# Short products and the group norm's remainder put at other places of a block of 256 tokens

## The chip, the cores and the metric

The kernel runs on 1 of the 8 cores of a Trainium2 chip. The metric is the device time of one execution in microseconds (us), the median of the runs.

## What is computed

One layer on 4096 tokens of 1024 features. `h` is the RMS-normalised input with a scale and a shift; one projection `h @ w_in` feeds a pooling branch and an RWKV-7 branch; the branches, each with a SiLU gate, are concatenated, go through `w_out`, are added to `x`, and a last RMSNorm follows. The RWKV branch, with 8 heads of 64, is the part that matters here:

```
r, w_lo, k, v, a_lo, z = split(seg)              # after a token shift
decay = exp(-exp(-softplus(-(w0 + tanh(w_lo) @ w_up)) - 0.5))
a  = sigmoid(a0 + a_lo @ a_up)
kk = normalise(k * k_k);  k = k * (1 + (a - 1) * k_a)
S_t = S_{t-1} (diag(decay_t) - kk_t^T (a_t kk_t)) + v_t^T k_t;   y_t = S_t r_t
y  = (y - mean) * rsqrt(var + eps) * ln_w + ln_b      # per head: the group norm
y_rwkv = (y + sum(r * k * r_k) * v) * silu(z)         # the sum is the bonus
```

## The kernel before

A first phase (to about 400 us) computes `h` and the pooling branch. The second, which the change touches, takes the tokens in 16 blocks of 256, each of 4 chunks of 64, and a last one projects with `w_out`.

In the second phase two things run side by side. **front(b+1)** (L536) prepares the next block. It computes 17 segments of the projection (`seg`, L550), 24 products of 128x257 each, into PSUM tiles `pj` of a pool of three buffers; segment 0 is `lo`, and each head pair p = 0 to 3 has four: 1+4p is k (`kS`), 2+4p r (`rS`), 3+4p v (`vS`), 4+4p z (`zS`). Tiles are called by segment here: pj_9 is the k segment of pair 2. The two operations at L561 (ScalarE) and L562 (VectorE) empty a `pj`. Front is a generator; `fill(n)` runs n of its steps, three products each, between the parts of the current block. Between the steps of a segment it also issues short products, from lists in `mid` by step number:

- `lowrank` (L588): products `pl` and `pa` (L591, L592), ScalarE's tanh `tw` and `ta` and an addition (L593 to L595), VectorE's scan `L` (L596), two exponentials `Ppad` and `Pi` (L597, L598). It runs in the v segment.
- `bonus` (L632): product `pb` (L634), then `bon` (L635). It needs `rk` (L615).
- `cent` (L622): products `vps` (L625) and two copies (L627). It needs `vS` only.

Their PSUM tiles come from the pool of `pj` too. For the last pair the two are left over in `f["todo"]` and run in `scores` of the next block.

**The current block** runs `scores` (L649; products `scp_0` to `scp_3` at L663, their masking at L670, copies at L678), `inverse` (L698; VectorE's recurrence of 30 pairs L727, L732 from the transposition `Ab`, L709, to the transpositions `UV`, `MQ`, L745, L746; then `qp`, L756, and `m21p`, L764, on TensorE, behind 20 steps of front and the product `lead`, L790), and `chain` (L796). In each chunk chain runs L815 with the state `S`, copies `xa` (L822), products `psn` (L827), copies `UV` (L835), the state's product `psn` (L843) with its renewal (L849), the output's product (L854) and copies `y` (L861).

After two chunks `gn` (L868) normalises y: square, sum (L871 to L874), a power on GpSimd (L876), the norm's product (L878), and `gn_out` (L885): four transpositions `ytp` (L890), copies `mx` (L892), two operations (L893, L894) and a DMA. gn is a generator of three parts; `run(gns[0], 1)` runs the next part where it stands. `ytp` shares a pool of two PSUM buffers with `scp_sc`, `d2p`, `btp` and `qp`.

Tile's scheduler sets the order of each engine's instructions: by the order of the code, with some parts moved ahead by 400 places (`tc.high_priority(offset=PRI)`), and an instruction that can't run yet by the scheduler's own account gives way to a later one. Each engine then runs its list strictly in this order.

Of the kernel before, what the change touches and what calls it, by code (L numbers as in the profile page):

```python
# [52 lines left out]
def kernel(  # L53
# [426 lines left out]
    with ExitStack() as ph:  # L480
# [56 lines left out]
        def front(b, f):  # L537
# [7 lines left out]
                    hx += [ht[:, k, :] for k in range(4)]  # L545


            mid = {3: [], 6: []}

            def seg(m, name, bufs=2):  # L550
                pp = ps_pj.tile([P, TB2 + 1], F32, tag="pj", name=f"pj{b}_{m}")
# [25 lines left out]
            for p in range(NPAIR):  # L577
# [19 lines left out]
                    A.activation(Pp[:, :, 1:], c3(L), AF.Exp, bias=0.0, scale=cexp)  # L597
                    A.activation(Pi, L, AF.Exp, bias=0.0, scale=-cexp)  # L598

                mid[3].append(lowrank)  # L600
                yield
                vS = yield from seg(3 + 4 * p, "vS")
                if p == 0:
# [36 lines left out]
                        PE.matmul(pn[32 * q : 32 * q + 32, :], hsel, sqs[q], start=True, stop=True)  # L640
                    A.copy(ssb, pn)

                mid[6] += [cent, bonus]
                if p < NPAIR - 1:
                    yield
            f["todo"] = [norms] + mid[6]
# [2 lines left out]
        def scores(b, f, fill):  # L649
            AR, BK = f["AR"], f["BK"]  # L650

            d2 = sm.tile([64, NI], F32, tag="d2", name=f"d2_{b}")
            d2T = sm.tile([P, 32], F32, tag="d2T", name=f"d2T{b}")
            sc = blk.tile([P, NI, P], F32, tag="sc", name=f"sc{b}")
            BT = blk.tile([P, NCH, 512], F32, tag="BT", name=f"BT{b}")
            stg = f["stg"] = f["UV"][0:64].rearrange("q c e -> q (c e)")[:, 0:1024].rearrange("q (t i) -> q t i", t=32)
            for ch in range(NCH):

                pts = [pool.tile([P, 512], F32, tag=tg, name=f"scp{b}_{ch}_{tg}") for pool, tg in ((ps_sc, "sc"), (ps_x, "px"))]
                for j in range(4):  # L660
                    for hq in range(2):
                        o = 64 * hq
                        PE.matmul(  # L663
                            pts[hq][:, j * P : (j + 1) * P],
                            BK[o : o + 64, j, ch].rearrange("q a t -> q (a t)"),
                            AR[o : o + 64, j, ch].rearrange("q a t -> q (a t)"),
                            start=True, stop=True,
                        )
                for hq in range(2):
                    V.tensor_mul(  # L670
                        sc[:, ch * NH : (ch + 1) * NH, :].rearrange("q (j h) t -> q j h t", h=2)[:, :, hq],
                        pts[hq].rearrange("q (j t) -> q j t", j=4),
                        mask.unsqueeze(1).to_broadcast([P, 4, P]),
                    )

                for kb in range(2):
                    o, i8 = 32 * kb, slice(ch * NH, (ch + 1) * NH)
                    A.copy(stg[o : o + 32, :, i8], sc[o : o + 32, i8, o : o + 32].rearrange("q i t -> q t i"))  # L678
                fill(FS + 1)
                if ch == 2:  # L680
                    pt = ps_sc.tile([P, 512], F32, tag="sc", name=f"d2p{b}")
                    for c_ in range(NCH):
                        PE.transpose(pt[:64, c_ * P : (c_ + 1) * P], ssb[:, c_ * C : (c_ + 1) * C], ident)
                    V.tensor_scalar_max(
                        d2.rearrange("q (c p h) -> q c p h", c=NCH, h=2),
                        pt[:64].rearrange("q (c p e) -> q c p e", c=NCH, e=32)[:, :, :, 0:2], L2_EPS * L2_EPS,
                    )
                    V.reciprocal(d2, d2)
                    for g in range(2):
                        V.transpose(d2T[64 * g : 64 * g + 64], d2)  # L690
                if ch != 2:
                    f["todo"].pop(0)()
                fill(FS)
                if ch % 2 == 0:
                    run(gns[0], 1)
            f["sc"], f["BT"], f["d2T"] = sc, BT, d2T

        def inverse(b, f, fill):  # L698
# [71 lines left out]
        def ordered(mm):  # L770

            pin[0] = True
            return tc.keep_in_program_order(mm)
# [22 lines left out]
        def chain(b, f, fill):  # L796
            AR, UV, sc, BT, pc = f["AR"], f["UV"], f["sc"], f["BT"], f["pc"]
            MT = UV[0:64].rearrange("q c (h t) -> q (c h) t", h=NH)
            pe, po = f["px"]
            uo = 4 * HS  # L800
            for ch in range(NCH):
                par = 256 * (ch % 2)

                psn = ps_s.tile([P, 512], F32, tag="psn", name=f"psn{b}_{ch}")
                if ch % 2 == 0:
                    y = blk.tile([P, 512], F32, tag="y", name=f"y{b}_{ch}", bufs=3)
                yv = y[64 * (ch % 2) : 64 * (ch % 2) + 64].rearrange("q (j f e) -> q j f e", f=2, e=HS)
                uv = UV[0:64, ch, :].rearrange("q (j f e) -> q j f e", f=2, e=HS)

                for p in range(NPAIR):  # L810
                    cs = slice(par + p * HS, par + (p + 1) * HS)
                    for ar in range(2):
                        for hf, px in ((0, pe), (1, po)):
                            o, ro = 64 * hf, 64 * (hf ^ ar)
                            ordered(PE.matmul(  # L815
                                px[ro : ro + 64, cs], AR[o : o + 64, p, ch, ar, :], S[o : o + 64, p, :],
                                start=(p == 0 and ar == 1), stop=(ar == 0), skip_group_check=True,
                            ))
                xa = blk.tile([64, 2, 256], F32, tag="W", name=f"xa{b}_{ch}")
                for hf, px in ((0, pe), (1, po)):  # L820
                    with tc.high_priority(offset=PRI):
                        A.copy(xa[:, hf, :], px[64 * hf : 64 * hf + 64, par : par + 256])  # L822
                fill(FA)
                nl = lead(b, f, ch + 1) if ch + 1 < NCH else iter(())
                for p in range(NPAIR):
                    for hf in range(2):
                        ordered(PE.matmul(  # L827
                            psn[64 * hf : 64 * hf + 64, uo + p * HS : uo + (p + 1) * HS],
                            MT[:, ch * NH + 2 * p + hf, :], xa[:, hf, p * HS : (p + 1) * HS],
                            start=True, stop=True, skip_group_check=True,  # L830
                        ))
                    run(nl, 1)
                for hf in range(2):
                    with tc.high_priority(offset=PRI):
                        A.copy(uv[:, :, hf], psn[64 * hf : 64 * hf + 64, uo:].rearrange("q (j e) -> q j e", e=HS))  # L835
                run(gns[0], 1)

                Sd = blk.tile([P, NPAIR, HS], F32, tag="Wt", name=f"Sd{b}_{ch}")
                V.tensor_mul(Sd, S, pc[:, :, ch : ch + 1].to_broadcast([P, NPAIR, HS]))
                fill(FB)  # L840
                for h in range(NH):
                    o, e = 64 * (h % 2), slice(h * HS, (h + 1) * HS)
                    ordered(PE.matmul(  # L843
                        psn[o : o + 64, (h // 2) * HS : (h // 2 + 1) * HS], BT[:, ch, e], UV[:, ch, e],
                        start=True, stop=True, skip_group_check=True,
                    ))
                with tc.high_priority(offset=PRI):
                    for p in range(NPAIR):
                        V.scalar_tensor_tensor(  # L849
                            S[:, p, :], psn[:, p * HS : (p + 1) * HS], pc[:, p, ch : ch + 1], Sd[:, p, :], op0=ALU.mult, op1=ALU.add,  # L850
                        )
                for h in range(NH):
                    hf, o = h % 2, 64 * (1 - h % 2)
                    ordered(PE.matmul(  # L854
                        (pe, po)[hf][o : o + 64, par + (h // 2) * HS : par + (h // 2 + 1) * HS],
                        sc[:, ch * NH + h, 64:128], UV[:, ch, h * HS : (h + 1) * HS],
                        start=False, stop=True, skip_group_check=True,
                    ))
                for hf, px in ((0, pe), (1, po)):
                    o = 64 * (1 - hf)  # L860
                    A.copy(yv[:, :, hf], px[o : o + 64, par : par + 256].rearrange("q (j e) -> q j e", e=HS))  # L861
                run(gns[0])
                if ch % 2 == 1:
                    gns[0] = gn(b, f, ch // 2, y)
                    run(gns[0], 1)
                fill(FY)
# [49 lines left out]
        def run(g, n=100000):  # L916
            for _ in range(n):
                if next(g, run) is run:
                    return
# [48 lines left out]
        gns = [iter(())]  # L968
        fs = {0: {}}
        run(front(0, fs[0]))  # L970
        for b in range(NB2):
            f = fs[b]
# [80 lines left out]
```

## Time and profile before

| | |
|---|---|
| median of 3 runs | 2112.47 us (2110.70 to 2113.29) |
| the profiled execution, its own time | 2114.03 us |
| its span, first to last instruction | 2112.3 us |
| TensorE busy (PE) | 1979.8 us, 94%, 20186 matmuls |
| VectorE (DVE) / ScalarE (ACT) / GpSimd (POOL) | 1404.4 / 1045.7 / 130.8 us |
| granted TensorE clock, mean | 0.984 |
| the chain of work that ended last | PE 47%, DVE 31%, ACT 13% |

A matmul's busy time in the profile includes its way through the array, so back-to-back matmuls overlap: a 128x257 product is shown with 0.27 us and the next one starts 0.11 us later. The PE column is therefore full while PE's idle times, shown in brackets, are short of the truth by the overlap. "L843 <- ACT UV L835" says what ended an idle time. A clock of 1.00 is 2.4 GHz, 0.50 is 1.2 GHz.

### The profile page before, as it was taken

Reading aid. Unit: us, or ns where it says so; the run is one execution under the profiler, and the core shown is the slowest. Engines: PE = TensorE matmul, PEld = TensorE weight load, DVE = VectorE, ACT = ScalarE, POOL = GpSimd, SP = SyncE. Lnnn points to the kernel's source line nnn. Section 1 sums busy time; section 2 is a strip of 40 time slices with the busy share of each in tenths; the row PEclk is TensorE's granted clock in tenths of the full one; section 3 lists DMA queues with packets and bytes.
Section 4 is the critical chain, followed back from the end, with each engine's and each line's share of the span. In section 5 each row is a group of like instructions: output and inputs, shape, how many; then the busy total and the mean of one; then the engine's idle time right before and its main releaser. Section 6 shows DMA issues by size and latency. Waiting matters only on the chain.

```text
span 2112.3 us, 48406 instructions
## 1 busy us (share of the span) xinstructions
PE 1979.8 (94%) x20186; PEld 1460.1 (69%) x20186; DVE 1404.4 (66%) x3533; ACT 1045.7 (50%) x2247; POOL 130.8 (6%) x262
## 2 busy tenths in 40 slices
PE   5999999999999999999999999999999989999998
PEld 2444444687777777777777777777777767788886
DVE  7898987466857757668577676685675766533333
ACT  3555433355565565655655656556556553322211
POOL 0000000000000000000000000000000000100000
PEclk8999999999999999999999999999999999999999
DMA  8867767200110110101101101011011334433422
GB/s 311 277 224 240 241 216 271 68 21 2 32 32 2 31 27 7 32 4 30 32 2 31 27 7 32 3 30 32 2 31 31 131 112 139 165 136 133 155 96 74
DMA packets 140445, 183.20 MB, mean 87 GB/s; under 512 B 12097, under 2 KB 94017, under 8 KB 140226
## 3 DMA queue, kind: packets, MB, share of 16 engines
q1 hardware_dynamic: 140226, 180.11, 25.9%
q8 instruction: 158, 2.59, 0.5%
q14 instruction: 61, 0.50, 0.1%
HBM read 121.22 MB, written 58.85 MB: 85 GB/s over the span
## 4 chain that ended last, share of the span: by engine, by line
PE 47%; DVE 31%; ACT 13%; issue 4%; DMA 2%; POOL 1%; SPq 0%; ACTq 0%; DVEq 0%; POOLq 0%
PE po L953 6%; PE po L955 6%; PE po L954 6%; DVE Wt L727 5%; DVE W L732 4%; PE pp L412 4%; PE pp L411 4%; PE pp L410 4%; PE pj L557 3%; PE pj L558 2%; PE pj L559 2%; DVE sc L670 2%; PE scp_sc L663 2%; DVE L L596 2%; ACT UV L678 2%
## 5 line engine op out<-in xcount | busy, mean ns | idle before, releaser
L557 PE MATMUL pj<-hh,w2h 128*128 128x257 f16 x2176 | 604.3, 278 | 14.3 <-DVE kS L562 13.5
L559 PE MATMUL pj<-hh,w2l 128*128 128x257 f16 x2176 | 598.1, 275 | 0.0
L558 PE MATMUL pj<-hl,w2h 128*128 128x257 f16 x2176 | 596.6, 274 | 0.0
L557 PEld LDWEIGHTS <-w2h 128*128 128x128 f16 x2176 | 213.1, 98 | 69.1 <-issue 27.4
L558 PEld LDWEIGHTS <-w2h 128*128 128x128 f16 x2176 | 215.6, 99 | 47.8 <-issue 17.0
L559 PEld LDWEIGHTS <-w2l 128*128 128x128 f16 x2176 | 211.7, 97 | 31.7
L953 PE MATMUL po<-wo,mh 128*128 128x512 f32 x512 | 204.6, 400 | 2.4 <-ACT mh L937 2.4
L954 PE MATMUL po<-wo,mh 128*128 128x512 f32 x512 | 202.1, 395 | 0.0
L411 PE MATMUL pp<-lo,w1h 128*128 128x512 f16 x512 | 194.0, 379 | 1.4 <-DVE lo L225 1.4
L410 PE MATMUL pp<-hi,w1h 128*128 128x512 f16 x512 | 194.1, 380 | 0.6 <-ACT hi L224 0.6
L412 PE MATMUL pp<-hi,w1l 128*128 128x512 f16 x512 | 194.0, 379 | 0.0
L957 DVE TENSOR_TENSOR x<-po,x 128x512 f32<-128x512 f32 x64 | 44.2, 691 | 155.8 <-PE po L955 155.7
L959 ACT ACTIVATE sq<-x 128x512 f32<-128x512 f32 x64 | 40.4, 631 | 212.0 <-DVE x L957 194.9
L727 DVE TENSOR_TENSOR Wt<-W,Ab 128x30 f32<-128x30 f32 (+7 forms) x480 | 118.5, 247 | 13.7 <-ACT Ab L711 3.1
L732 DVE TENSOR_TENSOR W<-W,Wt 128x30 f32<-128x30 f32 (+7 forms) x480 | 117.9, 246 | 8.8
L953 PEld LDWEIGHTS po<-wo,mh 128*128 128x128 f32 x512 | 97.0, 189 | 24.6 <-ACT mh L937 2.6
L954 PEld LDWEIGHTS po<-wo,mh 128*128 128x128 f32 x512 | 96.8, 189 | 22.2
L678 ACT COPY UV<-sc 32x256 f32<-32x256 f32 x128 | 81.5, 637 | 48.4 <-DVE sc L670 46.3
L955 PE MATMUL po<-wo,ml 128*128 128x512 f32 x256 | 101.6, 398 | 0.0
L562 DVE SCALAR_TENSOR_TENSOR kS<-pj,c,kS 128x256 f32<-128x256 f32 x64 | 30.2, 471 | 103.4 <-ACT kS L561 102.9
L412 PEld LDWEIGHTS <-w1l 128*128 128x128 f16 x512 | 50.1, 98 | 61.6 <-issue 2.0
L410 PEld LDWEIGHTS <-w1h 128*128 128x128 f16 x512 | 50.2, 98 | 59.0 <-issue 0.8
(244 smaller groups left out, 3815.1 us busy)
## 6 DMA issues: line engine op xcount, KB each, us to landing
x<-in_x_dram SPq DMA_DIRECT2D x64, 256.0 KB, 3.1
out_dram<-x SPq DMA_DIRECT2D x64, 256.0 KB, 2.0
xk<-in_xT_dram SPq DMA_DIRECT2D x56, 256.0 KB, 4.1
xt<-in_x_dram SPq DMA_DIRECT2D x28, 512.0 KB, 5.7
wada<-in_w_ada_dram SPq DMA_DIRECT2D x24, 512.0 KB, 6.7
w2raw<-in_w_in_dram SPq DMA_DIRECT2D x17, 512.0 KB, 6.0
hh<-hT_hi SPq DMA_DIRECT2D x32, 257.0 KB, 4.1
hl<-hT_lo SPq DMA_DIRECT2D x32, 257.0 KB, 3.3
```

The source lines that it names most:

```text
L410: PE.matmul(pp, w1_hi[m][:, k, :], hi, start=(k == 0), stop=False)
L411: PE.matmul(pp, w1_hi[m][:, k, :], lo, start=False, stop=False)
L412: PE.matmul(pp, w1_lo[m][:, k, :], hi, start=False, stop=(k == KT - 1))
L557: unpin(PE.matmul(pp, w2_hi[m][:, k, :], hh[k], start=(k == 0), stop=False))
L558: PE.matmul(pp, w2_hi[m][:, k, :], hl[k], start=False, stop=False)
L559: PE.matmul(pp, w2_lo[m][:, k, :], hh[k], start=False, stop=(k == KT - 1))
L678: A.copy(stg[o : o + 32, :, i8], sc[o : o + 32, i8, o : o + 32].rearrange("q i t -> q t i"))
L727: V.tensor_mul(tmp[:, :n, :k], W[:, r0:, k : k + 1].to_broadcast([P, n, k]), Ab[:, k : k + 1, :k].to_broadcast([P, n, k]),)
L732: V.tensor_add(W[:, r0:, :k], W[:, r0:, :k], tmp[:, :n, :k])
L953: unpin(PE.matmul(po, mh[:, k, ts_], wo[0][k][n], start=(k == 0), stop=False))
L954: PE.matmul(po, mh[:, k, ts_], wo[1][k][n], start=False, stop=False)
L955: PE.matmul(po, (ml[:, k] if b % 2 == 0 else ml[k])[:, ts_], wo[0][k][n], start=False, stop=(k == KT - 1))
```

## The change

Four edits, by line numbers of before: `lowrank` runs at step 5 of the v segment, not 3; `bonus` at step 6 of the next k segment and `cent` in the next r segment, not the other way round; in scores, the leftover norms and bonus run in chunk 0 and the leftover cent in chunk 1, and both remaining parts of the last group norm run in chunk 0, not in chunks 0 and 2; in chain, the next part of the group norm is issued behind the state's renewal, not ahead of `Sd` (L839), and the third part is no longer run at the end of chunk 2 but behind the renewal of chunk 3. Lines L839 to L854 of before are one lower or the same after (the state's product is L842, its renewal L848).

```diff
-            mid = {3: [], 6: []}
+            mid = {5: [], 6: []}
...
-                mid[3].append(lowrank)
+                mid[5].append(lowrank)
...
-                mid[6] += [cent, bonus]
+                mid[6] += [bonus, cent]
...
-                if ch != 2:
+                for _ in range((2, 1, 0, 0)[ch]):
                     f["todo"].pop(0)()
                 fill(FS)
-                if ch % 2 == 0:
-                    run(gns[0], 1)
+                if ch == 0:
+                    run(gns[0])
...
-                run(gns[0], 1)
 
                 Sd = blk.tile([P, NPAIR, HS], F32, tag="Wt", name=f"Sd{b}_{ch}")
...
+                run(gns[0], 1)
                 for h in range(NH):
...
-                run(gns[0])
                 if ch % 2 == 1:
+                    run(gns[0])
                     gns[0] = gn(b, f, ch // 2, y)
```

What the scheduler makes of it shows at three places. VectorE at the end of the inverse, before:

```order
L743 TENSOR_TENSOR W_12972<-W_12972,d2T_12820 128x512
L839 TENSOR_TENSOR Sd_0_13683<-S,pc_11630 128x256
L745 STREAM_TRANSPOSE UV_11631<-W_12972 64x16x32 x2
L562 SCALAR_TENSOR_TENSOR kS_9_13393<-pj_9_13357,c_103,kS_9_13393 128x256
L746 STREAM_TRANSPOSE MQ_13420<-UV_11631 32x1024
L635 TENSOR_TENSOR bon_12846<-pb_1_13437,vS_7_13294 128x256
L562 SCALAR_TENSOR_TENSOR rS_10_13446<-pj_10_13404,c_103,rS_10_13446 128x256
```

and after the change:

```order
L743 TENSOR_TENSOR W_12972<-W_12972,d2T_12820 128x512
L610 TENSOR_TENSOR ta_1_13244<-ta_1_13244,kS_5_13193 128x256
L745 STREAM_TRANSPOSE UV_11631<-W_12972 64x16x32 x2
L612 TENSOR_TENSOR BK_13098<-ta_1_13244,Pi_1_13246 128x4x64
L746 STREAM_TRANSPOSE MQ_13418<-UV_11631 32x1024
L615 SCALAR_TENSOR_TENSOR rk_1_13306<-rS_6_13240,pv,ta_1_13244 128x256
L562 SCALAR_TENSOR_TENSOR zS_8_13345<-pj_8_13314,c_103,zS_8_13345 128x256
L562 SCALAR_TENSOR_TENSOR kS_9_13391<-pj_9_13357,c_103,kS_9_13391 128x256
L635 TENSOR_TENSOR bon_12846<-pb_1_13382,vS_7_13294 128x256
L620 SCALAR_TENSOR_TENSOR szt_12847<-tz_1_13348,zS_8_13345 128x256
L838 TENSOR_TENSOR Sd_0_13681<-S,pc_11630 128x256
```

Five operations that stood ahead of L746, namely rk_1, the emptying of pj_8 and pj_9 (zS_8, kS_9), szt and Sd, now stand behind it.

TensorE at the same time, after the change (before, all 32 products of qp stand behind L790, one and a half segments further on, and the row behind pj_9 is that of pj_10):

```order
L559 LDWEIGHTS w2l_1763
L559 MATMUL pj_9_13357<-hh_1_12841,w2h_1762 128x257
L756 MATMUL qp_13543<-MQ_13418,sc_12821 32x32 x13
L634 MATMUL pb_1_13382<-rk_1_13306,bones 128x256
L557 LDWEIGHTS w2h_1766
L557 MATMUL pj_10_13402<-hh_0_12837,w2h_1766 128x257
```

Thirteen products of qp, which read MQ, and pb_1, which reads rk_1, now stand ahead of segment 10, of which before 18 products and more ran while VectorE was still at the inverse.

ScalarE in chunk 2 of the chain, before:

```order
L822 COPY xa_2_13844<-px_1_13534 64x4x64
L593 ACTIVATE tw_3_13786<-pl_3_13850,pv 128x256
L594 ACTIVATE ta_3_13787<-pa_3_13851,pv 128x256
L595 ACTIVATE tw_3_13786<-tw_3_13786,one 128x256
L597 ACTIVATE Ppad_3665<-L_3_13788 128x4x64
L598 ACTIVATE Pi_3_13789<-L_3_13788 128x256
L835 COPY UV_11631<-psn_2_13826 64x4x64 x2
```

and after:

```order
L835 COPY UV_11631<-psn_2_13826 64x4x64 x2
L593 ACTIVATE tw_3_13786<-pl_3_13876,pv 128x256
L594 ACTIVATE ta_3_13787<-pa_3_13877,pv 128x256
L595 ACTIVATE tw_3_13786<-tw_3_13786,one 128x256
L597 ACTIVATE Ppad_3665<-L_3_13788 128x4x64
L598 ACTIVATE Pi_3_13789<-L_3_13788 128x256
L861 COPY y_2_13827<-px_0_13533 64x4x64
```

The copies UV, for which the state's product waits, now stand ahead of the lowrank part of pair 3, and the copies y of chunk 2 behind its exponentials.

## Rows read from the trace of the kernel before

**Rows 1.** Stretches of a block's length: us, busy by engine, PEclk, DMA.
```profile
521.24:605.87 84.63, 78.86 (x1060) 62.66 (x1060) 58.58 (x168) 50.14 (x115) 5.94 (x11) 0.98 0.08 20
605.87:689.43 83.56, 77.71 (x1060) 61.83 (x1060) 58.60 (x168) 49.93 (x115) 5.94 (x11) 1.00 0.08 21
...
sum 1095.87, PE 1020.58 PEld 811.55 DVE 761.94 ACT 650.49 POOL 77.22; mean PE 78.51 PEld 62.43 DVE 58.61 ACT 50.04 POOL 5.94
```

**Rows 2.** The same columns for four stretches of one block.
```profile
1035.80:1052.57 16.77, 16.61 (x191) 13.46 (x190) 10.87 (x25) 10.62 (x23) 1.64 (x1) 1.00 0.32 84
1052.57:1085.20 32.63, 29.45 (x241) 24.11 (x241) 31.04 (x98) 17.23 (x37) 1.63 (x7) 1.00 0.01 3
1085.20:1091.14 5.94, 5.65 (x44) 4.31 (x44) 3.67 (x9) 3.34 (x8) 0.85 (x2) 1.00 0.01 3
1091.14:1120.36 29.22, 27.08 (x587) 20.63 (x587) 13.02 (x37) 18.94 (x49) 1.82 (x2) 0.94 0.03 7
```

**Rows 3.** Who waited for whom, whole span: total us, times, longest.
```profile
PE psn L843 <- ACT UV L835: 25.2, 16, 1.7
```

**Rows 4.** TensorE in time, chunk 2 of the chain: start, us, instruction, [idle before].
```profile
1113.08 0.69 PE L843 MATMUL psn<-UV,BT 128*64 128x64 f32 x16 [1.66 <-ACT UV L835]
...
1114.83 0.42 PE L557 MATMUL pj<-hh,w2h 128*128 128x257 f16 x1
1115.04 0.42 PE L558 MATMUL pj<-hl,w2h 128*128 128x257 f16 x1
```

**Rows 5.** VectorE in time, the same place.
```profile
1110.35 0.69 DVE L878 TENSOR_TENSOR y<-y,rstd 128x512 f32<-128x512 f32 x1 [1.75 <-POOL rstd L876]
```

**Rows 6.** ScalarE in time, the same place.
```profile
1111.67 0.42 ACT L597 ACTIVATE Ppad<-L 128x256 f32<-128x256 f32 x1 [1.59 <-DVE L L596]
...
1112.30 0.73 ACT L835 COPY UV<-psn 64x256 f32<-64x256 f32 x2
```

**Rows 7.** VectorE in time, in the inverse.
```profile
1056.42 0.19 DVE L727 TENSOR_TENSOR Wt<-W,Ab 128x30 f32<-128x30 f32 x1 [0.22 <-ACT Ab L711]
1056.64 0.19 DVE L732 TENSOR_TENSOR W<-W,Wt 128x30 f32<-128x30 f32 x1
...
1057.32 0.22 DVE L727 TENSOR_TENSOR Wt<-W,Ab 128x56 f32<-128x56 f32 x1
1057.45 0.48 DVE L562 SCALAR_TENSOR_TENSOR rS<-pj,c,rS 128x256 f32<-128x256 f32 x1
...
1064.89 0.48 DVE L615 SCALAR_TENSOR_TENSOR rk<-rS,pv,ta 128x256 f32<-128x256 f32 x1
...
1083.57 0.48 DVE L562 SCALAR_TENSOR_TENSOR kS<-pj,c,kS 128x256 f32<-128x256 f32 x1
1083.97 1.22 DVE L746 STREAM_TRANSPOSE MQ<-UV 32x1024 f32<-32x1024 f32 x1
```

**Rows 8.** TensorE in time, from the start of segment 10 to the product lead.
```profile
1079.89 0.27 PE L557 MATMUL pj<-hh,w2h 128*128 128x257 f16 x1
...
1084.11 0.27 PE L557 MATMUL pj<-hh,w2h 128*128 128x257 f16 x1 [0.97 <-DVE kS L562]
...
1085.56 0.70 PE L591 MATMUL pl<-lo,up 64*128 64x256 f32 x2 [0.29 <-DVE bon L635]
...
1091.14 0.68 PE L790 MATMUL px<-UV,sc 64*64 64x64 f32 x16
1091.75 0.75 PE L756 MATMUL qp<-MQ,sc 32*32 32x32 f32 x64
```

**Rows 9.** Groups by line: busy us, mean ns of one, idle before.
```profile
L678 ACT COPY UV<-sc 32x256 f32<-32x256 f32 x128 | 81.5, 637 | 48.4 <-DVE sc L670 46.3
L892 ACT ACTIVATE mx<-ytp,pv 128x128 f32<-128x128 f32 x128 | 47.8, 450 | 4.2 <-PE ytp L890 3.5
...
L670 DVE TENSOR_TENSOR sc<-scp_sc,mask 128x512 f32<-128x512 f32 x64 | 43.9, 686 | 17.8 <-PE scp_px L663 17.4 <-PE scp_sc L663 0.4
L876 POOL TENSOR_TENSOR rstd<-var,nhalf 128x8 f32<-128x8 f32 x32 | 53.3, 1665 | 477.9 <-DVE var L874 477.9
```

## Prediction

> **What bounds the kernel now.** I read the stretches of a block's length first. Between the same wait of two neighbouring blocks lie 84.63 or 83.56 us, and over 13 of them 1095.87 us, so 84.30 on average [rows 1]. The change touches nothing else that is long: 15 blocks carry a front, the last one and the projection behind it are filled with other work. A change of 1 us per block is thus 15 us or 0.7% of the whole, and a measurement of this kernel can tell 0.2%, about 4.2 us, from no change. The two lengths go with the clock: the short blocks have 1.00, the long ones 0.98 [rows 1], and the slow clock costs 84.63 - 83.56 = 1.07 us of a block.
>
> Then I cut one long block of 84.56 us into four stretches at places that every block passes [rows 2]: from the state's product of chunk 3 through scores to the start of the inverse, **A**, 16.77; from there to the end of L746 (MQ), **B**, 32.63; to the product lead, L790, **C**, 5.94; to the state's product of the next chunk 3, **D**, 29.22. In B VectorE is busy for 31.04 of 32.63 us, so it ends B; in A, C and D TensorE is busy nearly throughout and its waits count.
>
> Last the order of events in D. TensorE waits 1.66 us at 1113.08 for the copies UV [rows 4], once in each of the 16 blocks [rows 3]. ScalarE makes these copies behind Ppad, for which it idled 1.59 us until the scan L had come from VectorE [rows 6]; and VectorE had the scan behind the norm's product, for which it idled 1.75 us until GpSimd's power had come [rows 5]. Behind that wait the 128x257 products start 0.21 us apart instead of 0.11 [rows 4]: the clock has fallen to its lower level, and D as a whole shows 0.94 [rows 2].
>
> **The change, stretch by stretch**, against the block of 84.56 us.
>
> *D.* The copies UV now stand ahead of the lowrank part, so they wait for nothing but their product. The same TensorE work without the wait (nine products of front, psn, pl and pa, six products, from L815 of this chunk at full pace) ends at about 1110.8 instead of 1113.08: 2.3 us. The slow clock behind it goes as well, and two short products and three of the four transpositions move to elsewhere in the block: another 1.7; 13 of the 32 products of qp behind the lead go to C, 0.28. Something is late in their place. The lowrank part comes later, the scan stands behind the norm's product on VectorE as before, and the copies y of this chunk stand behind Ppad and Pi on ScalarE; L815 of chunk 3 writes the PSUM buffers that these copies empty and waits for them, by my reckoning 1.1 us. D: -2.3 - 1.7 - 0.28 + 1.1, about -3.2 (bounds -4.3, if the copies y are in time, and -2.1, if that wait is twice as long).
>
> *A.* The four copies mx of the first group norm now come in chunk 3 ahead of the last copies y, 1.5 us in a row (0.45 each, overlapping) [rows 9]. That delays the square, the sums and the power of the second group norm, 1.67 us on GpSimd [rows 9]; the norm's product is done 8.0 us behind the start of A, and TensorE has ytp behind it in its list. From there: ytp 0.5, four mx 1.5, L893 and L894 and two maskings 0.6 apart each (0.69 with overlap) [rows 9], the emptying of lo and the small work on d2 1.5, two maskings 1.3, two copies of 0.64 [rows 9]: 8.0 + 0.5 + 1.5 + 2.4 + 1.5 + 1.3 + 1.3 = 16.5. What leaves is that L893 and L894 no longer split the last maskings. A: 16.5 to 16.9 against 16.77, taken as 0. The scheduler also puts four products of scp_1 for one half of the heads and four for the other in a row, where halves alternated; no row shows eight such in a row, so A is bounded by -1.5 (its DVE waits go and nothing comes) and +1.5.
>
> *B.* Five operations leave it for the place behind L746. The kS one occupies 0.40 us, from 1083.57 to 1083.97 [rows 7], and the others are of its kind and size: -1.9. They were good neighbours, though. An L732 that stands directly behind its L727 starts 0.22 us after it, for 0.19 us of work; where a foreign operation stands between, that one starts 0.13 after an L727 of 0.22 [rows 7]. So each place between two dependent operations saves some 0.12 us, and of 26 such places taken before, 21 are left: +0.6. Lowrank two steps later and bonus ahead of cent I cost at nothing on VectorE, since its list reaches them behind the recurrence, after their products; without that cover it is the 0.5 us of two short products later, inside A's bounds. B: -1.3 to -1.6, taken as -1.4. The Trainium skill, VectorE: DVE Perf Modes, section The DRAIN you can't avoid, says that the flush behind each operation can't be skipped by leaving out the waits; by it the five lost places would cost nothing, B would be -1.9, and the sum about 8 us lower. The rows contradict it with 0.12 us a place, and the sum goes by the rows.
>
> *C.* This is where the time comes back. Of TensorE's list thirteen products of qp, which read MQ, now stand ahead of pb_1 and of segment 10. Segment 10 needs the PSUM buffer of segment 8, which VectorE empties behind L746. So all that before ran from the start of segment 10 at 1079.89 to L790 at 1091.14, 11.25 us, much of it under the inverse, now starts only when MQ is there. From it go the waits of 0.97 and 0.29 us and their overlap, 0.17 each [rows 8]: 9.65. To it come pb_1, 0.45, and 13 of 32 products of qp of 0.69 (1091.75 to the next at 1092.44), 0.28 [rows 8]: C becomes 10.4 instead of 5.94, +4.4. TensorE arrives there early: it also waits at pb_0, because rk_0 is not ready when it comes. In the order of before VectorE makes rk_0 at 1064.89 [rows 7] and TensorE comes to pb only one segment later; now it comes 1.8 us too soon. Counted from there, TensorE has 101 products at 0.11 and 2.0 of short ones, 13.2 us, and VectorE 16.1 us of work until MQ (from 1064.89 + 0.48 to 1085.20, less the 2.0 of the five operations and less 1.7 of recurrence that now stands ahead of rk_0): TensorE idles about 2.9 us at qp.
>
> *The clock.* A wait of 1.66 us brought it down in 9 of the 13 blocks (those of the longer kind, 1095.87 = 13 x 83.56 + 9 x 1.07). One of 2.9 should do so nearly always, and behind it TensorE has no slack: at 0.21 instead of 0.11 us for some 16 products, +1.5. The wait at pb_0 will do so in some blocks; there TensorE has slack until qp, but VectorE comes to depend on it: +0.6 on average (bounds of both together 0 and +3.5).
>
> *Sum per block:* A 0, B -1.4, C +4.4, D -3.2, clock +2.1: +1.9 on the block of 84.56, so 86.46. Against the average of 84.30 that is +2.16, and over 15 blocks +32.4 us. The profiled execution took 2114.03 us, 1.56 more than the median of 2112.47; the sum is 2146.4 for it and **2145.0** for the median.
>
> **The rivals.**
> 1. *The wait at qp is covered and D's gain stands (faster).* The place is the start of the inverse. Without L893, L894 and bon between the last maskings, the inverse could begin 2 us earlier relative to TensorE, if the norm's product isn't late in A; the whole rest moves with it and the clock stays up. For it: VectorE works only 10.87 of A's 16.77 us [rows 2], so there is room. Against it: the power of 1.67 us and the copies mx stand in A's chain [rows 9]. Per block A -2.0, B -1.4, C +4.4, D -3.2, clock +0.1: -2.1, or -1.84 against the average; 2112.5 - 27.6 = 2085. It decides from the point where A is under 15.3 us. Chance 0.20.
> 2. *The clock stays up* in spite of the new waits: the sum without its term is -0.2 on 84.56, +0.06 against the average, so 2113.4. For it: 4 of 13 blocks kept the full clock behind the wait of 1.66 us [rows 1]. Against it: the new wait is nearly twice as long. Chance 0.12, of which 0.09 lies within 0.2%.
> 3. *Two slow stretches in every block.* The wait of 1.8 us at pb_0 brings the clock down too, the emptying of segments 5 and 6 comes late, and VectorE, which must take its list in order, loses 1.4 us in B on top, and the clock's term is 2.7 instead of 2.1: +3.9 on 84.56, +4.16 against the average, 2175. For it: a wait of 1.66 did so in most blocks. Against it: part of the slow time falls under VectorE's own work. Chance 0.13. The Trainium skill, TensorE: Matmul & The Clock Gate, section HAM oscillation, describes a loop in which a wait of every pass brings the clock down in every pass; by it this rival would be the likeliest. The trace shows it for 9 of 13 passes only.
>
> **How the numbers follow.** The forecast of 2145.0, with its own range of 2123 to 2162 (C and the clock at their bounds), has 0.55. It lies slower; rival 3 too; rival 2 has 0.02 slower, 0.01 faster and 0.09 the same; rival 1 is faster. Faster 0.21, same 0.09, slower 0.70. The range reaches down to 2092, most of the way into rival 1 (A's bound of -1.5 alone is 22 us), and up to 2172, just short of rival 3; about 0.1 is left out at either end.
>
> **What would show it.** Right: in the stretch from MQ to lead some 10 us instead of 5.94; TensorE waiting for MQ at L756, each time over 2 us, and for rk at L634; no wait of L842 for UV of over 0.3 us; L815 waiting for the copies y; D near 26 us; clock falls in the inverse, not in D. Wrong: L756 with no wait for MQ, or A shorter than 15.3 us (rival 1); PEclk of 1.00 in whole blocks (rival 2); blocks of over 88 us (rival 3).

## The result and the profile after

The change is slower: 2174.61 us, median of 4 runs (2173.24 to 2177.98), against 2112.88 us of before in the same comparison. The ratio is 1.0295, interval 1.0277 to 1.0313. The forecast was 2145.0 us with a range of 2092 to 2172: the sign was right, the size half of the measured loss, and the time lies 2.6 us outside the range.

The stretches of the prediction, in one block of the change (us, busy by engine with the number of instructions for PE, PEld, DVE, ACT and POOL, then PEclk, DMA share, GB/s):

```profile
973.80:991.25 17.45, 17.45 (x181) 14.18 (x181) 12.24 (x28) 12.27 (x27) 1.64 (x1) 1.00 0.32 89
991.25:1022.47 31.22, 25.95 (x219) 21.35 (x217) 29.50 (x93) 15.33 (x32) 1.33 (x7) 1.00 0.00 1
1022.47:1035.76 13.29, 13.24 (x108) 10.17 (x108) 4.95 (x13) 4.73 (x12) 0.91 (x2) 0.75 0.00 1
1035.76:1062.55 26.79, 25.13 (x557) 19.21 (x556) 12.61 (x37) 17.64 (x46) 1.82 (x2) 1.00 0.02 5
```

The same four of a block of before whose clock stayed at 1.00 (the block of rows 2 had the slow stretch in D):

```profile
1120.36:1137.22 16.86, 16.69 (x191) 13.54 (x190) 10.87 (x26) 10.63 (x23) 1.64 (x1) 1.00 0.31 84
1137.22:1169.84 32.62, 29.46 (x241) 24.11 (x241) 31.03 (x98) 17.23 (x37) 1.63 (x7) 1.00 0.01 3
1169.84:1175.78 5.94, 5.65 (x45) 4.31 (x44) 3.66 (x9) 3.34 (x8) 0.85 (x2) 1.00 0.02 4
1175.78:1203.92 28.14, 25.93 (x588) 19.87 (x587) 13.02 (x37) 18.73 (x49) 1.82 (x2) 1.00 0.05 11
```

The block of the change takes 88.75 us in all, this one of before 83.56. Nearly all the loss is in C, from MQ to lead: 5.94 became 13.29 us. B gave 1.40 back, D 1.35 (2.4 where before had the slow stretch), A grew by 0.6. Over 14 blocks the change took 1242.18 us and before 1182.08:

```profile
530.44:1772.62 1242.18, 1143.97 (x14841) 908.32 (x14841) 830.23 (x2338) 699.40 (x1610) 79.76 (x154) 0.96 0.09 26
```

```profile
530.17:1712.25 1182.08, 1099.87 (x14842) 874.44 (x14841) 820.52 (x2338) 700.40 (x1610) 83.16 (x154) 0.99 0.10 28
```

That is 60.1 us, and the spans (2171.5 and 2112.3) differ by 59.2. TensorE's waits have changed places (who waited for whom: total, times, longest):

```profile
PE qp L756 <- DVE MQ L746: 48.9, 15, 3.3
PE pb L634 <- DVE rk L615: 25.6, 15, 1.7
PE px L815 <- ACT y L861: 10.7, 15, 0.7
...
PE psn L842 <- ACT UV L835: 0.7, 2, 0.4
```

The wait for UV [rows 3] is gone. TensorE waits at pb_0 and at qp instead, and at L815 for the copies y. What stands behind the wait at qp (start, us, instruction, idle before):

```profile
1022.52 0.63 PE L756 MATMUL qp<-MQ,sc 32*32 32x32 f32 x26 [3.25 <-DVE MQ L746]
1023.08 1.22 PE L634 MATMUL pb<-rk,bones 128*128 128x256 f32 x2
1024.10 0.42 PE L557 MATMUL pj<-hh,w2h 128*128 128x257 f16 x1
1024.31 0.42 PE L558 MATMUL pj<-hl,w2h 128*128 128x257 f16 x1
```

The products of segment 10 start 0.21 us apart, as behind the old wait [rows 4]: the clock is at 1.2 GHz. Over C the mean is 0.75, so about half of its 13.29 us (2 x 0.25 x 13.29 = 6.6) ran at the lower level; TensorE is busy for 13.24 of them, so a quarter of C, 3.3 us, is lost to the clock. In D of before the mean of 0.94 over 29.22 us [rows 2] makes 3.5 us at the lower level, and not in every block. In the change the mean over C is 0.75 or 0.76 in each of the 14 blocks.

### The profile page after: what moved, and what is told of

It reads as the page before. It is cut to its first block, busy times and chain, and to the rows that moved or that the text cites. A ratio compares the mean times of both kernels' runs of the same rounds, so it can differ in the third digit from the quotient of the medians.

```text
span 2171.5 us, 48458 instructions
## 1 busy us (share of the span) xinstructions
PE 2026.2 (93%) x20186; PEld 1495.4 (69%) x20186; DVE 1413.5 (65%) x3533; ACT 1044.2 (48%) x2247; POOL 125.5 (6%) x262
## 4 chain that ended last, share of the span: by engine, by line
PE 55%; DVE 30%; ACT 9%; issue 4%; DMA 1%; SPq 0%; POOL 0%; ACTq 0%; DVEq 0%; POOLq 0%
PE po L953 5%; PE po L955 5%; PE po L954 5%; DVE W L732 5%; DVE Wt L727 4%; PE pj L557 4%; PE pp L412 4%; PE pp L410 4%; PE pp L411 4%; PE pj L558 4%; PE pj L559 4%; DVE sc L670 2%; PE pb L634 2%; PE psn L827 2%; DVE L L596 2%
## 5 line engine op out<-in xcount | busy, mean ns | idle before, releaser
L557 PE MATMUL pj<-hh,w2h 128*128 128x257 f16 x2176 | 615.2, 283 | 0.8 <-ACT up L425 0.8
L559 PE MATMUL pj<-hh,w2l 128*128 128x257 f16 x2176 | 608.4, 280 | 0.0
L558 PE MATMUL pj<-hl,w2h 128*128 128x257 f16 x2176 | 606.8, 279 | 0.0
L557 PEld LDWEIGHTS <-w2h 128*128 128x128 f16 x2176 | 217.3, 100 | 67.2 <-issue 21.2
L558 PEld LDWEIGHTS <-w2h 128*128 128x128 f16 x2176 | 219.7, 101 | 35.0 <-issue 5.2
L953 PE MATMUL po<-wo,mh 128*128 128x512 f32 x512 | 203.9, 398 | 0.0
L562 DVE SCALAR_TENSOR_TENSOR rS<-pj,c,rS 128x256 f32<-128x256 f32 x64 | 30.8, 481 | 153.4 <-ACT rS L561 153.4
L732 DVE TENSOR_TENSOR W<-W,Wt 128x30 f32<-128x30 f32 (+7 forms) x480 | 119.0, 248 | 11.6
L953 PEld LDWEIGHTS po<-wo,mh 128*128 128x128 f32 x512 | 96.4, 188 | 22.4 <-ACT mh L937 0.4
L955 PE MATMUL po<-wo,ml 128*128 128x512 f32 x256 | 101.7, 397 | 0.0
L627 ACT COPY UV<-vps 64x256 f32<-64x256 f32 x128 | 46.8, 366 | 94.3 <-PE vps L625 92.9
```

The source lines that it names most:

```text
L557: unpin(PE.matmul(pp, w2_hi[m][:, k, :], hh[k], start=(k == 0), stop=False))
L558: PE.matmul(pp, w2_hi[m][:, k, :], hl[k], start=False, stop=False)
L559: PE.matmul(pp, w2_lo[m][:, k, :], hh[k], start=False, stop=(k == KT - 1))
L732: V.tensor_add(W[:, r0:, :k], W[:, r0:, :k], tmp[:, :n, :k])
L953: unpin(PE.matmul(po, mh[:, k, ts_], wo[0][k][n], start=(k == 0), stop=False))
L955: PE.matmul(po, (ml[:, k] if b % 2 == 0 else ml[k])[:, ts_], wo[0][k][n], start=False, stop=(k == KT - 1))
```

## The experiments

Each kernel was timed against before on the same chip; before took 2112.71 us beside experiments 1 to 4, 2114.50 beside 5 to 8 and 2114.03 beside 9 to 12, so up to 2 us of a difference between two experiments can come from that. Most are before with some edits of the change, since these can be made apart.

**1. Lowrank at step 5, nothing else.**

```diff
-            mid = {3: [], 6: []}
+            mid = {5: [], 6: []}
...
-                mid[3].append(lowrank)
+                mid[5].append(lowrank)
```

> Kernel before with one edit of the change: lowrank at step 5 instead of 3. It alone puts the copies UV of chunk 2 ahead of the lowrank part on ScalarE. Theory (each edit acts in a stretch of its own, and this one is all of D's gain): the wait of L843 for UV, 1.66 us in each of 16 blocks, falls under 0.4; the clock stays at its upper level; D 29.2 to some 26.8 us, the other stretches as before, A 16.8, B 32.6, C 5.9; the block 84.3 to some 82, the time 2112.9 - 15 x 2.3, about 2078 us. Rival (D's gain needs the group norm moved as well): D keeps a wait of over 1 us elsewhere and the time is 2105 to 2115 us.

Measured: 2078.79 us, ratio 0.9839 (0.9826 to 0.9851). It is the fastest of all the versions here.

```profile
939.77:956.62 16.85, 16.69 (x191) 13.53 (x190) 10.92 (x26) 10.63 (x23) 1.64 (x1) 1.00 0.29 76
956.62:989.02 32.40, 28.91 (x242) 24.29 (x243) 30.91 (x98) 17.06 (x37) 1.38 (x7) 1.00 0.01 3
989.02:994.30 5.28, 5.28 (x45) 4.05 (x43) 3.24 (x8) 3.27 (x8) 0.86 (x2) 1.00 0.00 2
994.30:1021.75 27.45, 26.26 (x588) 20.22 (x587) 13.62 (x38) 18.87 (x50) 1.82 (x2) 1.00 0.05 12
```

The total came out as expected, the split did not: D is 27.45, not 26.8, and C fell too. Of the 2.3 us per block some 1.6 are at equal clock (83.56 to 81.98), the rest is the slow stretch, which none of the 14 blocks has any more.

**2. The group norm's two parts in chunk 0 of scores, nothing else.**

```diff
-                if ch % 2 == 0:
-                    run(gns[0], 1)
+                if ch == 0:
+                    run(gns[0])
```

> Kernel before with one edit: both remaining parts of the last group norm in chunk 0 of scores. Theory (this edit alone moves VectorE's operations behind L746 and products of qp ahead of segment 10, and that is the whole loss): a wait of L756 for MQ of 3 us or more in each block with 6.8 us at the lower clock, C 5.9 to some 13 us, B 32.6 to 31.2, D as before with its wait of 1.66: the block some 90 us, the time 2112.9 + 15 x 5.8, about 2200 us (2180 to 2215). Rival (the loss comes from bonus ahead of cent or from the chain's edits, which change what segment 10 waits for): within 10 us of 2113.

Measured: 2128.44 us, ratio 1.0073 (1.0060 to 1.0087), between the theory and the rival.

```profile
957.69:973.76 16.07, 15.64 (x172) 12.56 (x172) 11.04 (x25) 10.75 (x22) 1.64 (x1) 1.00 0.32 84
973.76:1005.04 31.28, 27.49 (x227) 22.47 (x225) 29.69 (x93) 15.72 (x33) 1.57 (x7) 1.00 0.01 1
1005.04:1014.73 9.69, 9.63 (x81) 7.80 (x81) 5.40 (x15) 5.03 (x12) 0.91 (x2) 1.00 0.01 3
1014.73:1043.07 28.34, 26.00 (x586) 19.86 (x585) 13.22 (x37) 18.72 (x49) 1.82 (x2) 1.00 0.04 11
```

```profile
PE qp L756 <- DVE MQ L746: 28.2, 15, 1.9
PE psn L843 <- ACT UV L835: 25.2, 16, 1.7
```

The place was right: this edit alone lengthens C, by 3.75 us, and shortens B by 1.34. The size was wrong: C is 9.69, not 13, with a wait at L756 of 1.9 and a clock of 1.00 throughout. So 3.75 us of the change's 7.35 in C come with this edit alone, and the rest is something else. The old wait for UV is still there, 1.7 us in each block, but in 13 of the 14 blocks the clock does not fall behind it.

**3 and 4. The change without one edit**: without that of experiment 2, and without that of experiment 1.

> The change without its edit of the group norm in scores (parts in chunks 0 and 2, as before). Theory: C back at 5.9 us with no wait of L756, D 26.8 as in the change, A 16.8 to 17.4, B 32.6: the block 82 to 82.7, the time 2078 to 2090 us, faster than before. Rival (bonus ahead of cent and the chain's edits cost as much as the group norm's): 2140 us or more.

> The change without its edit of lowrank (step 3, as before). Here rk of pair 1 stands ahead of L746 and no product of qp ahead of segment 10, while kS_9, szt, Sd and bon stand behind it. Theory (C's price goes with the number of operations behind L746 and with the qp products in the list): C between 6 and 10 us, with a wait of L557 for an emptied buffer in place of L756's; D as before, 29.2, with its wait of 1.66: the time 2113 to 2150 us. Rival (any operation moved behind L746 costs the full wait): C 13 us and the time over 2190 us.

Measured: 2109.04 us (0.9981, 0.9972 to 0.9990) and 2125.75 us (1.0058, 1.0046 to 1.0070). Without the group norm's edit C is back, but A is longer than thought:

```profile
1034.09:1052.73 18.64, 18.07 (x196) 14.67 (x195) 12.23 (x27) 12.10 (x27) 1.64 (x1) 1.00 0.29 81
...
1085.34:1091.51 6.17, 6.17 (x48) 4.51 (x46) 3.48 (x9) 4.31 (x10) 0.86 (x2) 1.00 0.01 3
```

Neither theory had 2109: the other edits cost 30 us against lowrank alone (experiments 7 and 8). Without lowrank's edit C is 8.46, inside the theory's 6 to 10, and the time is inside its range:

```profile
834.56:843.02 8.46, 8.46 (x72) 6.91 (x70) 4.68 (x12) 4.85 (x12) 0.86 (x2) 1.00 0.00 0
```

And lowrank's edit, worth -34 us on the kernel before, costs 49 us here (2125.75 to 2174.61).

**5. The change with qp held behind lead**, VectorE's order kept:

```diff
-                    PE.matmul(pt[32 * q : 32 * q + 32, j * 32 : (j + 1) * 32], sc[0:32, i, 32:64], MQ[0:32, i, :], start=True, stop=True)
+                    ordered(PE.matmul(pt[32 * q : 32 * q + 32, j * 32 : (j + 1) * 32], sc[0:32, i, 32:64], MQ[0:32, i, :], start=True, stop=True))
```

> The change with all products of qp held behind the product lead, as before; VectorE's order stays that of the change. Theory (the five operations behind L746 are what costs, the place of qp is only where the wait shows): TensorE waits at pb_1 (L634) for rk_1 instead, 3.3 to 3.9 us, with the clock at its lower level behind it, C about 13.3 us, the time 2170 to 2185 us. Rival (the early products of qp cost): the wait shrinks to under 1.5 us, the clock stays up, C under 9 us, the time under 2120 us.

Measured: 2168.21 us, ratio 1.0254 (1.0240 to 1.0268), 2 us below the theory's 2170 to 2185. The wait stands at pb_1 now, 3.7 us for rk_1, which VectorE makes behind L746. So the early products of qp only show the wait. That VectorE's order makes it is what is left; no run put that order alone back. The wait, and C in two blocks of this kernel:

```profile
760.55 1.19 PE L634 MATMUL pb<-rk,bones 128*128 128x256 f32 x2 [3.72 <-DVE rk L615]
...
760.03:773.31 13.28, 12.76 (x83) 9.73 (x83) 4.96 (x14) 4.73 (x12) 0.92 (x2) 0.75 0.01 1
848.70:860.36 11.66, 11.14 (x83) 8.73 (x83) 4.96 (x14) 4.74 (x12) 0.91 (x2) 0.86 0.00 0
```

The same instructions, the same wait: a mean clock of 0.75 costs 1.62 us more than 0.86. Of the 14 blocks ten are of the longer kind (13.05 to 13.28 us) and four of the shorter (11.64 to 11.93), so 1.62 is the largest such difference.

**6 and 9. The wait filled.** Added products, which read W and whose result is overwritten by lead, keep TensorE at work while it would wait for VectorE; 14 in the one kernel and 3 in the other. The line that makes the tiles `px` moves ahead of them, and qp stands behind lead, as in experiment 5:

```diff
+                for _ in range(14):
+                    PE.matmul(f["px"][0], Wf[:, 0:P], Wf, start=True, stop=True, skip_group_check=True)
                 for g in range(2):
                     V.transpose(MT[:, :, 0:32].rearrange("c i (t g) -> c g t i", g=2)[:, g], W[64 * g : 64 * g + 64])
```

> The change with 14 products of 128x512 per block added that nothing uses; they read W and so start when L743 has made it, in the middle of segment 9 and inside the stretch in which TensorE waits for MQ; the products of qp stand behind lead, so the kernel to compare is that with qp behind lead. The added work is 14 x 0.23 = 3.2 us per block. Theory (half of C's price is the lower clock that the wait brings): no lower clock in C, no wait of over 1.5 us, C 10 to 11 us; the time falls, though work is added: 2174.6 - 15 x 2.8, about 2132 us (2115 to 2145). Rival (the clock's fall costs nothing, since VectorE sets the end of C anyway): 2170 us or more.

> As the kernel with the filled wait, but 3 added products instead of 14: one 128x512 product of W with itself took 2 x 0.43 us there, not 0.23, so the 14 took 12.0 us, where the wait held 3.3. Three take 2.6 us, inside the wait. To compare: the change with qp behind lead (2168.2 us, C 13.2 in the blocks with 6.8 us at the lower clock, 11.7 with 3.4). Theory (the lower clock behind the long wait is some 3 us of C): no lower clock in C, C 10.3 to 10.8 us, the block 85.9, the time some 2134 us (2125 to 2142), faster with work added. Rival (the wait itself, not the clock, is the price): C 13 us and the time 2160 us or more.

The first missed: 2286.86 us, because one such product counts as two instructions and takes 2 x 0.43 us, so the 14 outlast the wait by far and the time decides nothing:

```profile
1058.60 12.28 PE L746 MATMUL px<-W 128*128 128x512 f32 x28 [1.33 <-DVE W L743]
```

The clock stayed up in it, though. With three products the time is 2144.25 us (ratio 1.0145, 1.0130 to 1.0159), and C:

```profile
924.16:935.09 10.93, 10.68 (x91) 8.57 (x89) 5.04 (x13) 5.23 (x13) 0.91 (x2) 1.00 0.01 2
```

That is 24 us faster than experiment 5 with three products of 0.86 us added in every block, 2 us above the theory's range and far from its rival. C, 0.1 above its range, holds six more of front's products than in experiment 5 (some 0.7 us), which stood ahead of the wait there. So what C loses behind the long wait is the clock.

**7 and 8. Lowrank's edit with the chain's edits; with bonus ahead of cent and the leftover parts.**

> Kernel before with the lowrank edit and the chain's edits of the group norm (behind the renewal of S, third part in chunk 3); bonus, cent and the scores as before. Compared with lowrank alone (2078.8 us, blocks of 81.96) and with the change without its group norm edit in scores (83.80 per block). Theory (the chain's edits move ytp, mx, L893 and L894 of the first two chunks from D into A, where the path to the inverse is, ScalarE's and TensorE's): A 16.84 to some 18.2, D 27.44 to 26.8, the block 82.8 to 83.4, the time 2091 to 2100 us. Rival (bonus ahead of cent with its waits for rk costs it): 2076 to 2082 us.

> Kernel before with the lowrank edit, bonus ahead of cent and the leftover parts in chunks 0 and 1; the group norm as before. Theory (TensorE waits for rk at L634, but inside B, which VectorE ends anyway): B and C within 0.5 us of lowrank alone, A up by the 0.4 us of pb at most, the block 81.9 to 82.6, the time 2078 to 2090 us. Rival (the waits at L634 push C and the inverse): C over 6 us, B over 33 us, the time over 2100 us.

Measured: 2088.67 us (0.9875, 0.9862 to 0.9889) and 2103.68 us (0.9952, 0.9938 to 0.9965). The first:

```profile
939.90:958.24 18.34, 17.99 (x196) 14.59 (x195) 12.26 (x28) 12.02 (x27) 1.64 (x1) 1.00 0.30 83
...
995.93:1022.43 26.50, 25.12 (x582) 19.42 (x581) 12.38 (x36) 17.50 (x46) 1.82 (x2) 1.00 0.02 5
```

and the second:

```profile
948.14:965.49 17.35, 16.77 (x191) 13.60 (x190) 10.92 (x26) 10.59 (x23) 1.64 (x1) 1.00 0.28 74
...
998.11:1004.28 6.17, 6.17 (x49) 4.51 (x47) 3.48 (x9) 4.31 (x10) 0.85 (x2) 1.00 0.02 4
```

The chain's edits move 0.95 us out of D and put 1.5 into A, 2 us better than expected in time. Bonus ahead of cent costs more than expected, 14 us above the range: 0.5 in A, 0.2 in B and 0.9 in C, with two waits of TensorE at pb in each block (1.84 us for rk, and 1.51, which the profile puts down to L732). Little of that is in B, as the theory had it, but A and C grow by more than it allowed, and the time is the rival's (over 2100).

**10. Lowrank's edit and the group norm's in scores together.**

> Kernel before with two edits: lowrank at step 5, and both remaining parts of the group norm in chunk 0 of scores. Alone they give 2078.8 (blocks of 81.96) and 2128.4 us (85.36). Theory (they don't add up, because lowrank's edit delays VectorE's operations of pair 1 by two steps and the other edit starts the inverse ahead of them: seven operations of pair 1 and 2, ta and two BK and AR among them, stand behind L746 here): a wait for MQ or rk of 3 us or more, lower clock behind it, the time 2130 to 2185 us. Rival (the edits act in separate stretches and add up): 2112.7 - 33.9 + 15.7 = 2094.5, between 2088 and 2101 us.

Measured: 2121.93 us, ratio 1.0039 (1.0026 to 1.0052), between the theory and the rival, with a wait of 1.85 us instead of 3. C of two blocks:

```profile
665.88:677.02 11.14, 11.08 (x80) 8.43 (x80) 5.97 (x17) 4.66 (x12) 0.92 (x2) 0.85 0.01 1
751.83:761.30 9.47, 9.42 (x80) 7.59 (x80) 5.95 (x16) 4.65 (x12) 0.91 (x2) 1.00 0.01 2
```

and the first products of each, behind the same wait:

```profile
665.94 0.24 PE L756 MATMUL qp<-MQ,sc 32*32 32x32 f32 x2 [1.85 <-DVE MQ L746]
...
751.88 0.24 PE L756 MATMUL qp<-MQ,sc 32*32 32x32 f32 x2 [1.85 <-DVE MQ L746]
```

One fell, one didn't, and that is 1.67 us. Where the clock is 1.00 the block takes 84.28 us, and the two edits' parts (the table below) give 83.78, so they nearly add up; the falls, in 9 of the 14 blocks, put 1.1 us on the average block.

**11 and 12. Lowrank alone, at step 6 and at step 4.**

> Kernel before with lowrank at step 6 instead of 3 (5 in the first experiment). UV stands ahead of the lowrank part here too; rk_1, zS_8 and szt come later in VectorE's list than at step 5, all still ahead of L746 but Sd. Theory (what counts is that UV stands ahead and that few operations stand behind L746): within 8 us of step 5, 2072 to 2087 us. Rival (each step that lowrank is later delays VectorE's work and segment 10): over 2090 us.

> Kernel before with lowrank at step 4. On ScalarE UV of chunk 2 stands between Ppad and Pi, so it still waits for the scan L and thus for the group norm's power. Theory (UV's place behind Ppad is the whole of D's wait): the wait of L843 for UV stays between 0.9 and 1.6 us, the clock falls in some blocks, and the time is 2098 to 2113 us. Rival (the later products, not UV's place, give the gain): halfway between, or 2078 to 2097 us.

Measured: 2081.96 us (0.9848, 0.9834 to 0.9863) and 2099.02 us (0.9925, 0.9912 to 0.9939), both times as the theory had them; but at step 4 the clock stays at 1.00 in all 14 blocks, where the theory had it fall in some. At step 4 ScalarE still makes UV behind Ppad, and L843 waits 1.25 us for it:

```profile
1107.50 0.42 ACT L597 ACTIVATE Ppad<-L 128x256 f32<-128x256 f32 x1 [1.25 <-DVE L L596]
1107.82 0.73 ACT L835 COPY UV<-psn 64x256 f32<-64x256 f32 x2
...
1108.61 0.57 PE L843 MATMUL psn<-UV,BT 128*64 128x64 f32 x12 [1.25 <-ACT UV L835]
```

So with UV behind Ppad 20 of lowrank's 34 us are lost. Of the 14 that stay some 11 are the slow stretch (84.30 less 83.56, in 15 blocks). That all of the 20 belong to the place of UV is not shown, since C and B are shorter at step 5 too (the table below).

## Why the prediction was wrong, step by step

At a clock of 1.00 the stretches of the four parts, each as its difference, add up to the change within 0.6 us a stretch. The parts are lowrank (experiment 1 less before), the group norm in scores (2 less before), the chain (7 less 1), bonus and leftovers (8 less 1). C of the change is taken at 1.00, as 13.29 less the 3.3 that experiments 5 and 10 give (1.62 from 0.75 to 0.86, 1.67 from 0.85 to 1.00), which is also a quarter of it, by its mean clock.

| us per block | before | lowrank | norm in scores | chain | bonus | sum | the change |
|---|---|---|---|---|---|---|---|
| A | 16.86 | -0.01 | -0.79 | +1.49 | +0.50 | 18.05 | 17.45 |
| B | 32.62 | -0.22 | -1.34 | +0.01 | +0.22 | 31.29 | 31.22 |
| C at 1.00 | 5.94 | -0.66 | +3.75 | 0 | +0.89 | 9.92 | 10.0 |
| D | 28.14 | -0.69 | +0.20 | -0.95 | -0.13 | 26.57 | 26.79 |
| lower clock | | | | | | | +3.3 |

In C the agreement of 9.92 and 10.0 is in part chance: by the same columns the change without lowrank's edit would have 10.58 there, and experiment 4 has 8.46, so the parts of C hang on each other. Nor is the wait of 3.25 us that of one edit: it is 1.9 with the norm in scores alone and 1.85 with lowrank's edit beside it.

- **B was right.** Forecast -1.4, measured -1.40. The five operations left, and with them the places where they saved time; the norm's edit alone gives -1.34. That the sum came out to the hundredth is luck: lowrank and bonus, which it put at nothing, are -0.22 and +0.22. The prediction drew from the Trainium skill (VectorE: DVE Perf Modes, The DRAIN you can't avoid) that lost neighbours would cost nothing, B -1.9. But the section also says that a next operation which is not held starts earlier, and rows 7 agree with that (0.13 us behind the start of one of 0.22 us).
- **C without the clock was nearly right.** Forecast 10.4, measured 10.0. The wait at qp was put at 2.9 us and is 3.25; that at pb_0 at 1.8 and is 1.7. Experiment 2 shows the edit that makes most of C, and experiment 5 that the place of qp does not, which leaves VectorE's order. In one place the 10.4 was lucky: the 11.25 us of before already held pb_1 (at 1081.88), which the sum added again, and it left out the four products vps of cent, which stand in C now and are about as long (0.45 us at 1064.93).
- **The clock's term failed**, and it is the largest miss. It stood as +1.5 for the wait at qp (some 16 products at half pace) and +0.6 for that at pb_0, 2.1 in all. Measured: 3.3 behind qp, since the clock stays low for twice as long as after the old wait, and none at pb_0, where no block shows a fall. In 14 blocks that is 1.2 x 14 = 17 us of the miss, and the slow products cost the change 3.3 x 14 = 46 us, where before paid 9 x 1.07 = 10 us in 13. The bounds (0 to 3.5) held it, but the sum was taken from the old wait's length of slow time, and nothing in the trace of before showed what follows a wait twice as long.
- **D's gain was too large by 0.8**: -3.2 forecast, -2.43 measured against the 29.22 of rows 2. The step on UV was right. Chunk 2 up to the state's product takes 2.27 us less (from 1105.07 to 1113.08 before, 8.01; from 1050.53 to 1056.27 after, 5.74), where 2.3 was forecast, and L815's new wait is 0.72 instead of 1.1. From the state's product of chunk 2 to that of chunk 3 it is 6.28 instead of 7.28 us, with that wait of 0.72 in it, so the slow clock and the moved products do give the forecast's 1.7. What was missed lies right behind lead: from there to the first L815 pass 4.73 us (1035.76 to 1040.49) where before had 3.91 (922.98 to 926.89), and the prediction had put 0.28 less there. pb_2 now stands in the middle of m21p, 0.63 us:

```profile
1038.28 1.02 PE L764 MATMUL m21p<-UV,MQ 32*32 32x32 f32 x6
1039.23 0.70 PE L634 MATMUL pb<-rk,bones 128*128 128x256 f32 x2
1039.86 0.70 PE L764 MATMUL m21p<-UV,MQ 32*32 32x32 f32 x58
```

  The rest is mostly m21p's wait for the copies MQ, three of which ScalarE makes behind tz, which waits for zS from VectorE:

```profile
1037.81 0.42 ACT L619 ACTIVATE tz<-zS 128x256 f32<-128x256 f32 x1 [0.49 <-DVE zS L562]
1038.25 1.14 ACT L758 COPY MQ<-qp 32x256 f32<-32x256 f32 x3
```

  Before, tz stood ahead of all four copies, but came earlier, 1.26 us behind lead instead of 2.05:

```profile
924.24 0.42 ACT L619 ACTIVATE tz<-zS 128x256 f32<-128x256 f32 x1 [0.67 <-DVE zS L562]
924.68 1.53 ACT L758 COPY MQ<-qp 32x256 f32<-32x256 f32 x4
```

  In experiment 1, without pb_2 there, tz starts 1.82 us behind lead and the same stretch takes 4.47 us (994.30 to 998.77), so a late tz comes with lowrank's edit. This is read from the traces; no run took tz or pb_2 away.
- **A was 0.7 longer** than in rows 2 (17.45 against 16.77), inside the bounds of 1.5 but taken as 0, since the chain over the norm was to end it. TensorE is busy for all of A's 17.45 us, and the sum had no term for it. In it stand ytp of the chain, pb, and products scp_1 that no longer alternate between the halves of the heads:

```profile
1069.08 1.16 PE L663 MATMUL scp_px<-AR,BK 64*128 64x128 f32 x8
...
1071.59 1.16 PE L663 MATMUL scp_sc<-AR,BK 64*128 64x128 f32 x8
```

  Eight of one half take 1.09 us (1069.08 to 1070.17), 2.2 for all sixteen. Alternating, as before, all sixteen of a chunk take 1.10:

```profile
1043.08 0.37 PE L663 MATMUL scp_sc<-AR,BK 64*128 64x128 f32 x1
1043.09 0.37 PE L663 MATMUL scp_px<-AR,BK 64*128 64x128 f32 x1
...
1044.18 0.28 PE L557 MATMUL pj<-hh,w2h 128*128 128x257 f16 x1
```

  That no row showed such a run of eight, as the prediction had it, meant that its price was unknown. It does not lengthen A by itself: experiment 2 has such runs too (962.41, 964.57), and its A is 16.07. By experiment 7 the chain's edits are what lengthens A, by 1.49.
- **The rivals.** The time is that of the rival with two slow stretches (2175), but not its mechanism: B did not grow and the clock did not fall at pb_0. It is one slow stretch of twice the length. The sign set for it, blocks of over 88 us, came all the same (88.75), so it did not tell the two apart. The other rivals are out: L756 waits, and no block kept the clock at 1.00.

Together: clock +1.2, D +0.8, A +0.7, C -0.4 make the 2.3 us by which the forecast of +1.9 on the block of 84.56 was short of the measured 88.75.

## What to carry to other kernels

Price a new wait of TensorE by what the clock does behind it, not by its length alone: here a wait of 3.25 us cost as much again in slow products, while waits of 1.25 to 1.9 us left the clock alone in some kernels and blocks and not in others. Make the edits of such a change one at a time before judging it: one of the four is worth 1.6%, and the other three hid it. In an order that a scheduler sets, an edit in one place (the norm in scores) can put operations of quite another part (rk, zS, kS) behind the bottleneck's last instruction; look first at what stands behind that instruction.

## What was not expected of the hardware

- The same wait can bring the clock down or not. In experiment 10 a wait of 1.85 us in each block left it at 1.00 in 5 of 14; in experiments 2 and 8 waits of 1.9 and 1.8 us in each block did so in all 14. Before fell behind 1.66 us for UV in 9 of 13 blocks, and experiment 2, with the same wait, did not in 13 of 14. Waits over 3 us (the change and experiment 5) brought it down in every block. The Trainium skill (TensorE: Matmul & The Clock Gate, HAM oscillation) describes a loop whose wait, some 3 to 5 us for a DMA, brings the clock down in each pass. The change, with 3.25 us, agrees; the prediction had applied it to a wait of 1.8 us, and no block fell there. What decides for the shorter waits was not separated here.
- Behind a longer wait the lower clock mostly lasted longer: a mean of 0.75 over C against 0.85 in experiment 10, about 6.6 and 3.3 us (2 x 0.15 x 11.14). In four of experiment 5's 14 blocks it lasted half as long behind the same 3.72 us.
- Products of 64 rows on the two halves of the array ran side by side when they alternated: sixteen took 1.10 us, and eight of one half in a row took 1.09.
- A 128x512 product of float32 data cost 0.86 us here as two instructions; the last projection's products of the same shape, shown as f32 too, start 0.23 us apart (L953 to L955). Their operands are fp32r tiles.
